# Newton's steps of the reciprocal square roots moved from VectorE to GpSimd, in a hybrid decoder layer

## The chip, the core and the metric

The kernel runs on one core of a Trainium2 chip. The time is device microseconds of one execution of the whole program, from a run on the chip; lower is better. The engines are named as in the profile: PE (TensorE matmuls), PEld (its weight loads), DVE (VectorE), ACT (ScalarE), POOL (GpSimd), SP (SyncE, which here issues DMAs). Each engine runs its own list of instructions in order, and engines wait for each other by semaphores.

## What is computed

One layer of a decoder trunk on 2048 tokens of width 1024, in float32. The input is normalised and multiplied by one wide weight matrix; the columns of the result feed five groups of four heads of 64; each group's output is gated, the five are joined (width 1280), multiplied by an output matrix and added to the input:

```
h = rms_norm(x, norm_g)
proj = h @ w_in
ya = spatial_gating(...)          # A: gMLP, with an rms_norm over each head of v
yb = forgetting_attention(...)    # B: softmax attention, rms_norm over each head of q and k
yc = mlstm(...)                   # C: chunked matrix memory, rms_norm over each head of its output
yd = rwkv7_time_mix(...)          # D: delta rule; a norm over each head of k, rms_norm of its output
ym = memory_attention(...)        # M: attention to 256 memory tokens, rms_norm of q and k
out = x + concat(y * silu(z)) @ w_out
```

Every one of these norms needs a reciprocal square root of a small statistic: `y * rsqrt(mean(y * y) + eps)`.

## The kernel before

Each float32 product is made of three passes of a split number (a rounded part and a rest), so the weights and the activations are first split by ACT (L222, L329: the rounded part) and DVE (L225, L330: the rest). The work comes in three stretches. From 0 to about 950 us PE runs the input projections (L267, L289, L315) in blocks of 512 tokens, with the recurrent groups C and D between them. From about 950 to 1430 us attention B and M runs beside the projections of group A and of M. From there to the end PE runs the output projection (L879).

The source is written as generators that are stepped between groups of matmuls, and a scheduler that works on the written program sets the final order of each engine's list. The order is fixed when the program is built; at run time each engine keeps to its list.

`rsqrt` (L148 to L156) turns a small tile `t` in place into its reciprocal root. Line 152 makes a first guess from the bits of `t`, and three rounds of Newton's method follow (L154, L155, L156), every step needing the one before. The tiles are 128x8 mostly, some 128x4, 128x2 or 64x16. All of it stands on DVE: ten instructions a call. The two helpers `rq` (the guess `y` and the scratch `u`) are single buffers that all calls share.

The calls, 62 in all:
- `rstd` (L369) and `first` (L502): the statistic `ss` of the layer's input and of the memory tokens; PE spreads it by L383, or ACT uses it (L749).
- `head_norm` (L403): the statistic `rs` of the heads of q and k (then L413 on DVE scales, and PE transposes in L418), of group C (then L1683 on DVE), and of group A (then L715 on DVE). L401 is the sum before it, on DVE, and L397 the square, on ACT.
- group D: `rn` in the front part (L1311; PE spreads it by L1322) and `sy` in the back part (L1497; L1510 on DVE scales).

POOL has little else. In the first stretch these are small copies (L632, L634, L1297, L1373) and two products in each of the eight front parts of group D (L1315, L1333). In attention it adds up the exponentials: ACT writes a tile `pe` (L1087), and POOL adds it to `es` (L1099 the first two, L1101 the others), one list of adds for every block of 512 queries.

Of the kernel before, what the change touches and what calls it, by code (L numbers as in the profile page):

```python
# [13 lines left out]
ALU = mybir.AluOpType  # L14
# [106 lines left out]
def body(ctx: ExitStack, tc, x, xT, mem, memT, wp, wkv, wout, pv, wa, sguT, sgub, out, dbg=None):  # L121
    nc = tc.nc
    V, A, G, T, SY = nc.vector, nc.scalar, nc.gpsimd, nc.tensor, nc.sync
# [24 lines left out]
    def rsqrt(t):  # L148

        n, b = t.shape[0], t.base_partition() if callable(t.base_partition) else t.base_partition  # L150
        y, u = (cp.tile([P, 16], F32, tag=f"rq{i}", bufs=1, name="rq")[b:b + n, :t.free_size()] for i in range(2))
        V.tensor_scalar(y.bitcast(I32), t.bitcast(I32), -0.5, 1597463007.0, op0=ALU.mult, op1=ALU.add)
        for o in (y, y, t):
            V.tensor_tensor(u, y, y, op=ALU.mult)  # L154
            V.scalar_tensor_tensor(u, u, -0.5, t, op0=ALU.mult, op1=ALU.mult)  # L155
            V.scalar_tensor_tensor(o, u, 1.5, y, op0=ALU.add, op1=ALU.mult)  # L156


    hp2 = cp.tile([P, 16], F32, name="hp2")
# [22 lines left out]
    rctx = ExitStack()  # L182
    rp = rctx.enter_context(tc.tile_pool(name="rp", bufs=1, side="right"))
    rwkv = Rwkv(nc, rp, dr, lambda: bank("rw"), bank, ident, par, hp2, rsqrt, wa, dd, smd, mixd[3])

    cw = ctx.enter_context(ExitStack())
# [164 lines left out]
    def rstd(pool, tags, src, ntile):  # L351

        ss = mp.tile([P, 2, 4], F32, tag="ss", bufs=2, name="ss")
        xts = deque()
        lag = len(tags)
        for i in range(2 * ntile + lag):
            if i >= lag:
                j, xt = i - lag, xts.popleft()
                A.activation(xt, xt, AF.Square, accum_out=ss[:, j % 2, j // 2:j // 2 + 1])
            if i < 2 * ntile:  # L360
                tag, bufs = tags[i % lag]
                xts.append(pool.tile([P, Q], F32, tag=tag, bufs=bufs, name="xt"))
                SY.dma_start(xts[-1], src(i // 2, slice(i % 2 * Q, (i % 2 + 1) * Q)))
            if i >= lag - 1:
                yield
        r = ss[:, 0, :ntile]
        V.tensor_tensor(r, r, ss[:, 1, :ntile], op=ALU.add)
        V.tensor_scalar(r, r, 1.0 / DM, EPS, op0=ALU.mult, op1=ALU.add)
        rsqrt(r)  # L369
        yield  # L370
        return ss[:, 0]
# [22 lines left out]
    def head_norm(pt, n, eps, pool=None):  # L394

        sq = pool.tile([P, 3 + Q], F32, tag="cext", bufs=2, name="sq") if pool else xp.tile([P, 512], F32, tag="sq", bufs=2, name="sq")
        A.activation(sq[:, :n], pt, AF.Square)  # L397
        yield
        m = n // HD
        r = xp.tile([P, 8], F32, tag="rs", bufs=4, name="rs")  # L400
        V.tensor_reduce(r[:, :m], sq[:, :n].rearrange("q (u x) -> q u x", x=HD), axis=AX.X, op=ALU.add)  # L401
        V.tensor_scalar(r[:, :m], r[:, :m], 1.0 / HD, eps, op0=ALU.mult, op1=ALU.add)
        rsqrt(r[:, :m])  # L403
        yield
        yield
        yield
        return r[:, :m].rearrange("q (u o) -> q u o", o=1).to_broadcast([P, m, HD])
# [434 lines left out]
    op = att.c4.enter_context(tc.tile_pool(name="op", bufs=2, side="right"))  # L842
# [912 lines left out]
```

## Time and profile before

| what | value |
|---|---|
| median of three runs | 1740.68 us (1735.09 to 2513.16) |
| the profiled execution's own time | 1736.49 us |
| its span, first to last instruction | 1734.8 us |
| granted TensorE clock, mean | 0.975 of full |
| PE / DVE / ACT / POOL busy | 95% / 69% / 51% / 17% of the span |
| instructions on DVE / POOL | 2990 / 356 |

Matmuls are pipelined and their ends are modelled, so a busy PE is not a PE at its peak. The profile's idle times name what ended them. Equal instructions can have quite different durations, and in a list that is kept in order an instruction that waits holds up all behind it.

### The profile page before, as it was taken

Reading aid. Unit: us, or ns where it says so; the run is one execution under the profiler, and the core shown is the slowest. Engines: PE = TensorE matmul, PEld = TensorE weight load, DVE = VectorE, ACT = ScalarE, POOL = GpSimd, SP = SyncE. Lnnn points to the kernel's source line nnn. Section 1 sums busy time; section 2 is a strip of 40 time slices with the busy share of each in tenths; the row PEclk is TensorE's granted clock in tenths of the full one; section 3 lists DMA queues with packets and bytes.
Section 4 is the critical chain, followed back from the end, with each engine's and each line's share of the span. In section 5 each row is a group of like instructions: output and inputs, shape, how many; then the busy total and the mean of one; then the engine's idle time right before and its main releaser. Section 6 shows DMA issues by size and latency. Waiting matters only on the chain.

```text
span 1734.8 us, 31669 instructions
## 1 busy us (share of the span) xinstructions
PE 1641.8 (95%) x11306; PEld 1282.2 (74%) x11306; DVE 1196.9 (69%) x2990; ACT 881.3 (51%) x1895; POOL 302.3 (17%) x356
## 2 busy tenths in 40 slices
PE   7898999799999999999999999999999988999999
PEld 5676778687978888798888766667656655677887
DVE  7678685685977679488676887788687786752220
ACT  5566554544555455555444756566465646631110
POOL 5010000010100101010000045344444242100000
PEclk9999999899999999999999989999999999999999
DMA  6878654542453443344334544334334425654441
GB/s 198 256 230 259 184 161 97 139 145 86 135 157 101 132 141 115 86 134 146 98 101 141 167 120 130 105 102 130 96 86 110 113 68 137 191 162 114 143 130 56
DMA packets 200151, 234.36 MB, mean 135 GB/s; under 512 B 75016, under 2 KB 107336, under 8 KB 199992
## 3 DMA queue, kind: packets, MB, share of 16 engines
q1 hardware_dynamic: 185144, 218.69, 43.7%
q10 hardware_dynamic: 14848, 13.64, 2.6%
q8 instruction: 89, 1.46, 0.4%
q14 instruction: 70, 0.57, 0.1%
HBM read 180.44 MB, written 51.81 MB: 134 GB/s over the span
## 4 chain that ended last, share of the span: by engine, by line
PE 64%; DVE 16%; DMA 11%; ACT 4%; issue 3%; POOL 1%; SPq 1%; ACTq 0%; DVEq 0%; POOLq 0%
PE pj L315 14%; PE pj L879 12%; PE pj L267 12%; PE acc L1108 4%; DMA wraw<-in_wp 4%; PE pj L289 4%; DVE wt L225 2%; PE wk L1026 2%; PE p L1082 2%; PE p L1085 2%; PE rw L1359 1%; PE rw L1482 1%; PE rw L1484 1%; DVE ht L330 1%; DVE mx L1040 1%
## 5 line engine op out<-in xcount | busy, mean ns | idle before, releaser
L267 PE MATMUL pj<-ht,wt 128*128 128x512 f32 x1632 | 422.6, 403 | 5.8 <-DVE ht L330 2.7
L267 PEld LDWEIGHTS pj<-ht,wt 128*128 128x128 f32 x1632 | 298.3, 190 | 84.5 <-issue 10.5
L315 PE MATMUL pj<-wt,ht 128*128 128x256 f32 x2400 | 332.7, 290 | 9.3 <-ACT wt L222 3.4
L315 PEld LDWEIGHTS pj<-wt,ht 128*128 128x128 f32 x2400 | 304.9, 193 | 27.5 <-issue 7.4
L225 DVE TENSOR_TENSOR wt<-wraw,wt 128x512 fp32r<-128x512 f32 (+1 forms) x312 | 217.6, 700 | 78.0 <-ACT wt L222 76.4
L222 ACT CAST wt<-wraw 128x512 fp32r<-128x512 f32 (+1 forms) x312 | 184.8, 601 | 140.2 <-DMA wraw<-in_wp 92.5
L879 PE MATMUL pj<-wo,mt 128*128 128x512 f32 x960 | 231.3, 398 | 1.8 <-ACT wo L830 1.8
L879 PEld LDWEIGHTS pj<-wo,mt 128*128 128x128 f32 x960 | 180.2, 189 | 47.2 <-issue 2.4
L1101 POOL TENSOR_TENSOR es<-es,pe 128x512 f32<-128x512 f32 (+3 forms) x128 | 153.7, 1201 | 103.9 <-ACT pe L1087 98.9
L289 PE MATMUL pj<-ht,wt 128*128 128x512 f32 x480 | 138.9, 426 | 13.3 <-ACT wt L222 11.7
L1087 ACT ACTIVATE pe<-p 128x512 f32<-128x512 f32 x192 | 100.3, 541 | 50.3 <-PE p L1085 43.9
L1040 DVE TENSOR_REDUCE mx<-wk 128x1 f32<-128x512 f32 (+3 forms) x192 | 111.8, 614 | 18.2 <-PE wk L1026 14.3
L289 PEld LDWEIGHTS pj<-ht,wt 128*128 128x128 f32 x480 | 91.8, 200 | 39.1 <-ACT wt L222 12.1
L1108 PE MATMUL acc<-pe,v 128*64 128x512 f32 (+3 forms) x384 | 104.0, 594 | 6.3 <-DVE at L1141 6.3
L329 ACT ACTIVATE ht<-xr,pvt 128x512 fp32r<-128x512 f32 (+1 forms) x88 | 61.4, 703 | 61.9 <-DMA xr<-hbd 29.2
L1099 POOL TENSOR_TENSOR es<-pe 128x512 f32<-128x512 f32 (+1 forms) x32 | 43.2, 1351 | 246.3 <-ACT pe L1087 200.3
L1026 PE MATMUL wk<-ka,qb 66*128 66x512 f32 (+3 forms) x224 | 73.2, 383 | 10.2 <-DVE mx L1040 9.7
L1082 PE MATMUL p<-qa,kb 128*128 128x512 f32 x192 | 75.8, 396 | 5.8 <-ACT pe L1087 5.8
L330 DVE SCALAR_TENSOR_TENSOR ht<-xr,pvt,ht 128x512 fp32r<-128x512 f32 (+1 forms) x88 | 68.4, 784 | 16.8 <-ACT ht L329 16.1
L859 ACT CAST mt<-mr 128x256 fp32r<-128x256 f32 x80 | 31.6, 406 | 94.1 <-DMA mr<-mix 50.3
L1026 PEld LDWEIGHTS wk<-ka,qb 66*128 66x128 f32 x224 | 41.0, 196 | 49.3 <-DVE mx L1040 19.5
L1085 PE MATMUL p<-qb,ka 68*128 68x512 f32 x192 | 75.4, 395 | 0.0
(332 smaller groups left out, 2423.1 us busy)
## 6 DMA issues: line engine op xcount, KB each, us to landing
wraw<-in_wp SPq DMA_DIRECT2D x288, 256.0 KB
xr<-hbd SPq DMA_DIRECT2D x56, 256.0 KB
mr<-mix SPq DMA_DIRECT2D x80, 128.0 KB
xr<-in_x SPq DMA_DIRECT2D x32, 256.0 KB
out<-xr ACTq DMA_DIRECT2D x32, 256.0 KB
xt<-in_x SPq DMA_DIRECT2D x24, 256.0 KB
xr<-in_xT SPq DMA_DIRECT2D x24, 256.0 KB
hbd<-xr SPq DMA_DIRECT2D x24, 256.0 KB
```

The lines of the kernel that those rows point to most:

```text
L222: A.copy(wt[:, :, 0, :ncol], raw[:, :, :ncol])
L225: V.tensor_tensor(lo, raw[:, :, :ncol], wt[:, :, 0, :ncol].bitcast(F32), op=ALU.subtract)
L267: T.matmul(pt, wt[k // 2][:, k % 2, a, m * P:(m + 1) * P], hts[k][:, b, :], start=n == 0, stop=n == 3 * KT - 1)
L289: T.matmul(pts[m], wt[k // 2][:, k % 2, a, m * P:(m + 1) * P], hts[k][:, b, :], start=k + n == 0, stop=k == KT - 1 and n == 2)
L315: T.matmul(pt[:, ii * 256:ii * 256 + 256], hts[k][:, a, (i + ii) * P:(i + ii + 1) * P], wt[k // 2][:, k % 2, b, :], start=n == 0, stop=n = ...
L879: T.matmul(po, mts[i // 2, k][:, a, i % 2 * P:(i % 2 + 1) * P], wo[e * NK + k][:, b], start=n == 0, stop=n == 3 * NK - 1)
L1026: T.matmul(p1, self.qb[0:66, i * P:(i + 1) * P], self.k[kk][0][0:66, :w], start=True, stop=True, skip_group_check=diag)
L1040: V.tensor_reduce(*late.pop(), axis=AX.X, op=ALU.max)
L1082: T.matmul(p2[:, f:], kb[:, ks], self.qa[:, f:], start=True, stop=False)
L1085: T.matmul(p2[:, f:], ka[:, ks], self.qb[:, f:], start=False, stop=True)
L1101: G.tensor_tensor(self.sum[:, f:], self.sum[:, f:], e[:, f:], op=ALU.add)
L1108: self.att.nc.tensor.matmul(self.acc[64 * i:64 * i + 64, f:], self.v[:, kt], e[:, f:], start=kt < 2, stop=True, skip_group_check=True)
```

## The change

In `rsqrt` the first guess stays on DVE. The three rounds go to POOL, and since a round is written there as products and one multiply-add with two constants, it has four instructions instead of three: the square of the guess, its product with `t`, times -0.5 plus 1.5, and the product with the guess. A call is then one instruction on DVE and twelve on POOL.

```diff
         V.tensor_scalar(y.bitcast(I32), t.bitcast(I32), -0.5, 1597463007.0, op0=ALU.mult, op1=ALU.add)
         for o in (y, y, t):
-            V.tensor_tensor(u, y, y, op=ALU.mult)
-            V.scalar_tensor_tensor(u, u, -0.5, t, op0=ALU.mult, op1=ALU.mult)
-            V.scalar_tensor_tensor(o, u, 1.5, y, op0=ALU.add, op1=ALU.mult)
+            G.tensor_tensor(u, y, y, op=ALU.mult)
+            G.tensor_tensor(u, u, t, op=ALU.mult)
+            G.tensor_scalar(u, u, -0.5, 1.5, op0=ALU.mult, op1=ALU.add)
+            G.tensor_tensor(o, u, y, op=ALU.mult)
```

Lines below this place have a number that is higher by one in the changed kernel (L413 becomes L414). The scheduler makes a new order of the whole program. Three places of it follow.

DVE, at two calls of `head_norm` for q and k (tiles `rs` and `yn`) in the last block of the projections. Before:

```order
L152 TENSOR_SCALAR rq<-rs 128x8
L638 SCALAR_TENSOR_TENSOR qk<-cext,pvt,qk 128x512
L154 TENSOR_TENSOR rq<-rq 128x8
L1402 COPY xs<-x_125 128x256
L155 SCALAR_TENSOR_TENSOR rq<-rq,rs 128x8
L638 SCALAR_TENSOR_TENSOR qk<-cext,pvt,qk 128x512
L156 SCALAR_TENSOR_TENSOR rq<-rq 128x8
L154 TENSOR_TENSOR rq<-rq 128x8
L155 SCALAR_TENSOR_TENSOR rq<-rq,rs 128x8
L156 SCALAR_TENSOR_TENSOR rq<-rq 128x8
L154 TENSOR_TENSOR rq<-rq 128x8
L642 SCALAR_TENSOR_TENSOR qk<-cext,qk 128x512
```

And now:

```order
L402 TENSOR_REDUCE rs<-sq 128x8
L403 TENSOR_SCALAR rs<-rs 128x8
L152 TENSOR_SCALAR rq<-rs 128x8
L402 TENSOR_REDUCE rs<-sq 128x8
L403 TENSOR_SCALAR rs<-rs 128x8
L152 TENSOR_SCALAR rq<-rs 128x8
L414 TENSOR_TENSOR yn<-yn,rs 128x512 x2
L331 SCALAR_TENSOR_TENSOR ht<-xr,pvt,ht 128x512
L226 TENSOR_TENSOR wt<-wraw,wt 128x2x256 x2
```

The nine steps that lay among other work are gone from DVE. The scaling of `yn`, which needs their result, stands right behind the first guess of a second call, and that one needs the shared `rq` back from the first call.

POOL, near the end of attention, where it adds exponentials. Before:

```order
L1099 TENSOR_TENSOR es<-pe 128x512 x5
L1101 TENSOR_TENSOR es<-es,pe 128x512 x11
L1101 TENSOR_TENSOR es<-es,pe 128x384
L1101 TENSOR_TENSOR es<-es,pe 128x256
L1101 TENSOR_TENSOR es<-es,pe 128x128
L1099 TENSOR_TENSOR es<-pe 128x512 x3
```

And now:

```order
L154 TENSOR_TENSOR rq<-rq 128x8
L1102 TENSOR_TENSOR es<-es,pe 128x512
L155 TENSOR_TENSOR rq<-rq,rs 128x8
L1102 TENSOR_TENSOR es<-es,pe 128x512
L156 TENSOR_SCALAR rq<-rq 128x8
L157 TENSOR_TENSOR rq<-rq 128x8
L154 TENSOR_TENSOR rq<-rq 128x8
L155 TENSOR_TENSOR rq<-rq,rs 128x8
L156 TENSOR_SCALAR rq<-rq 128x8
L157 TENSOR_TENSOR rq<-rq 128x8
L1102 TENSOR_TENSOR es<-es,pe 128x512
L154 TENSOR_TENSOR rq<-rq 128x8
```

The steps of one call now stand in one list with the adds, and some adds stand between them.

PE, at the first front part of group D, where the statistic `rn` is spread over partitions. Before:

```order
L1300 MATMUL wk<-smp,w2r 128x256 x2
L1308 MATMUL wk<-bones,ag 128x2 x4
L278 MATMUL pj<-ht,wt 128x512
L267 MATMUL pj<-ht,wt 128x512 x30
L1322 MATMUL wk<-ident,rn 64x128 x8
L267 MATMUL pj<-ht,wt 128x512 x18
```

And now:

```order
L1309 MATMUL wk<-bones,ag 128x2 x4
L279 MATMUL pj<-ht,wt 128x512 x2
L268 MATMUL pj<-ht,wt 128x512 x11
L1323 MATMUL wk<-ident,rn 64x128
L268 MATMUL pj<-ht,wt 128x512 x4
L1323 MATMUL wk<-ident,rn 64x128 x4
L268 MATMUL pj<-ht,wt 128x512 x2
L1323 MATMUL wk<-ident,rn 64x128 x3
```

Between the sums that `rn` is made of and its first use 31 projection matmuls stood, and now 13 do.

## Rows read from the trace of the kernel before

**Rows 1.** The page, busy time of each engine, share of the span, instructions.

```profile
PE 1641.8 (95%) x11306; PEld 1282.2 (74%) x11306; DVE 1196.9 (69%) x2990; ACT 881.3 (51%) x1895; POOL 302.3 (17%) x356
```

**Rows 2.** The page, the chain that ended last, by engine.

```profile
PE 64%; DVE 16%; DMA 11%; ACT 4%; issue 3%; POOL 1%; SPq 1%; ACTq 0%; DVEq 0%; POOLq 0%
```

**Rows 3.** Stretches: busy us and instructions by engine, clock, DMA.

```profile
0.00:950.00 950.00, 897.72 (x7404) 745.41 (x7405) 696.16 (x2035) 501.88 (x1132) 93.04 (x184) 0.98 0.50 147
950.00:1430.00 480.00, 453.25 (x2543) 318.79 (x2543) 375.84 (x712) 284.59 (x557) 187.54 (x156) 0.96 0.41 113
```

**Rows 4.** Stretches, DVE busy with tile rq: all ten steps of the calls.

```profile
0.00:950.00 950.00, 82.98 (x460) 0.98 0.50 147
950.00:1430.00 480.00, 61.82 (x160) 0.96 0.41 113
```

**Rows 5.** Stretches, DVE busy with line L152 alone.

```profile
0.00:950.00 950.00, 7.57 (x46) 0.98 0.50 147
950.00:1430.00 480.00, 3.83 (x16) 0.96 0.41 113
```

**Rows 6.** Timeline of DVE, an undisturbed call: start, us, instruction.

```profile
281.16 0.17 DVE L152 TENSOR_SCALAR rq<-rs 128x8 int32<-128x8 int32 x1
281.37 0.17 DVE L154 TENSOR_TENSOR rq<-rq 128x8 f32<-128x8 f32 x1
...
283.17 0.69 DVE L413 TENSOR_TENSOR yn<-yn,rs 128x512 f32<-128x512 f32 x1
```

**Rows 7.** Timeline of DVE and POOL, a call in attention.

```profile
1419.63 1.12 DVE L154 TENSOR_TENSOR rq<-rq 128x8 f32<-128x8 f32 x1
1420.79 0.17 DVE L155 SCALAR_TENSOR_TENSOR rq<-rq,rs 128x8 f32<-128x8 f32 x1
...
1417.14 4.98 POOL L1101 TENSOR_TENSOR es<-es,pe 128x512 f32<-128x512 f32 x3 [6.61 <-ACT pe L1087]
```

**Rows 8.** Timeline of POOL: small and large, alone and dependent.

```profile
459.91 0.19 POOL L632 COPY cext<-ccy 128x3 f32<-128x3 f32 x1 [2.54 <-DVE rs L401]
1084.21 1.29 POOL L1101 TENSOR_TENSOR es<-es,pe 128x512 f32<-128x512 f32 x1 [0.51 <-ACT pe L1087]
1090.37 0.45 POOL L1101 TENSOR_TENSOR es<-es,pe 128x128 f32<-128x128 f32 x1 [2.11 <-ACT pe L1087]
1098.70 1.10 POOL L1099 TENSOR_TENSOR es<-pe 128x384 f32<-128x384 f32 x1 [1.49 <-ACT pe L1087]
1099.88 0.74 POOL L1101 TENSOR_TENSOR es<-es,pe 128x256 f32<-128x256 f32 x1
```

**Rows 9.** Groups by line and form: count, busy us, mean ns, idle before.

```profile
L632 POOL COPY cext<-ccy 128x3 f32<-128x3 f32 x16 | 7.5, 474 | 45.0 <-DVE qk L642 39.8 <-DVE rs L401 5.2
L225 DVE TENSOR_TENSOR wt<-wraw,wt 128x512 fp32r<-128x512 f32 x296 | 213.2, 723 | 78.0 <-ACT wt L222 76.4
L426 ACT COPY yn<-pj 128x512 f32<-128x512 f32 x24 | 14.0, 582 | 15.9 <-PE pj L315 11.7 <-DMA qk_Bk<-yn 4.1
L397 ACT ACTIVATE sq<-yn 128x512 f32<-128x512 f32 x25 | 15.8, 630 | 0.4
L401 DVE TENSOR_REDUCE rs<-sq 128x8 f32<-128x512 f32 x41 | 27.7, 680 | 17.1 <-ACT sq L397 16.9
L402 DVE TENSOR_SCALAR rs<-rs 128x8 f32<-128x8 f32 x41 | 12.1, 294 | 0.5
L413 DVE TENSOR_TENSOR yn<-yn,rs 128x512 f32<-128x512 f32 x25 | 18.0, 718 | 0.5
```

**Rows 10.** The chain that ended last: start, us, what.

```profile
861.51 11.10 PE pj L267 x48
```

**Rows 11.** Waits from 950 to 1430 us: total, times, longest.

```profile
POOL es L1099 <- ACT pe L1087: 98.4, 13, 10.6
POOL es L1101 <- ACT pe L1087: 97.0, 67, 6.6
```

**Rows 12.** Waits of PE: total us, times, longest.

```profile
PE wk L1322 <- DVE rn L156: 5.1, 5, 1.5
PE wk L418 <- DVE yn L413: 3.7, 4, 1.4
```

## The prediction

> **What bounds the kernel now.** I began with the page. PE is busy for 95% of the span and DVE for 69%, while POOL is busy for 17% [rows 1]. The reader should see an engine that is nearly full, a second one with a third of its time free, and a third one that is mostly empty. The chain of work that ended last is PE for 64% and DVE for 16% of the span; POOL has 1% [rows 2]. So time that is taken from DVE shows at the end only in part, and I use that 16% as its price below. The stretches show where there is room: PE has 52 us without work among the first 950 us and 27 us in attention, and POOL's 188 us in attention are 39% of that stretch, where the new work meets the most of its old work [rows 3].
>
> **What leaves DVE.** Nine of the ten steps of 62 calls. All ten steps take 83.0 us before 950 us and 61.8 us in attention [rows 4]; the first guesses, which stay, are 7.6 and 3.8 of that [rows 5]. So 75.4 and 58.0 us go, 133.4 us together. That is 0.16 us a step (75.4 over 9 x 46) in the first stretch, and 0.40 us (58.0 over 9 x 16) in attention. The reason is in two timelines. An undisturbed call runs at one step in 0.2 us, so nine steps last 1.8 us [rows 6]. In attention a step of the same size took 1.12 us while POOL was adding exponentials, and the next, 0.17 us [rows 7].
>
> **What POOL pays for a step.** POOL has no row of a product of 128x8, so I bound it. From below: a copy of three columns took 0.19 us, and the adds of 128 and of 512 columns, 0.45 and 1.29 us, lie on a line of 2.2 ns a column that begins at 0.17 and gives 0.19 us for 8 columns. A dependent add began 0.08 us after the end of the one before (1098.70 plus 1.10 is 1099.80, and the next starts at 1099.88) [rows 8]. That makes 0.27 us a step, 3.2 us for twelve, and 3.4 with a handover of 0.1 us on either side. No row has a multiply-add on POOL; I give it the price of the others. From above: the 16 copies of three columns took 0.47 us in the mean, beside a DVE that works on products of 0.72 us [rows 9]. That makes 0.55 us a step and 6.8 us a call. I take 4.5 us, near the low end: 3.4 plus three waits of half a product of DVE, 0.36 us each. The low end is nearer because DVE itself comes to a stop at the result, and from then on POOL works undisturbed.
>
> The Trainium skill, GPSIMD Engine Reference, section Engine selection, says that elementwise work belongs on VectorE, GPSIMD being about twice as slow with two inputs. Twice the 0.17 us of a DVE step would give a call of 6.3 us as an estimate, and by what follows an end near 1765 us. The trace bears the factor out for long operands (1.29 against 0.72 us for 512 columns) and not for the short copy (0.19 us), so I keep 4.5.
>
> **What DVE pays instead.** It now waits for POOL, in its own list. I went through the 62 calls in the new order and added up, by the mean durations of the trace, what DVE has to do between a first guess and whatever needs POOL next: the result, or the single shared `rq` for the next call's guess. Such a second guess comes after less than 4 us of other work in 13 calls (6 before); the DVE excerpt above has one. With a call of 4.5 us DVE arrives early in 32 of the 46 calls of the first stretch, by 93 us together, and in 14 of 16 in attention, by 48 us. Twelve adds of L1101 and two of L1099 stand between steps of these sixteen calls, for 14 x 1.37 = 19 us more (1.29 plus 0.08 [rows 8]). So DVE waits 93 + 48 + 19 = 160 us in place of 133 us of work: 27 us more, of which 16% is 4 us at the end. With 3.4 us a call the waits are 58 + 33 + 19 = 110 us, 23 us less than the work, which is 4 us off the end. With 6.8 us they are 169 + 82 + 19 = 270 us, 137 us more, or 22 us at the end. Behind a waiting DVE stand the splitting of weights (L225), that of activations (L330) and, in attention, the maxima; PE waits for all of these.
>
> **What PE pays.** In attention its order is the same. In the projections it comes to some users of the result earlier. At the first front part of group D 13 matmuls of 0.231 us [rows 10] are left, 3.0 us, to cover two small DVE steps, the call and a handover, some 5.0 us: PE waits 2 us. The other seven fronts keep at least 6.5 us of cover. For q and k the way from the projection's end is a copy, a square, a sum, its scaling, a guess, the call and the product: 0.58 + 0.63 + 0.68 + 0.29 + 0.17 + 4.5 + 0.72 = 7.6 us [rows 6, 9], and the shortest cover left is 8.3 us. That does, except where two calls stand close: at the place shown the second one starts 3.6 us late, so PE waits 3 us. The waits of before at these users, 5.1 and 3.7 us [rows 12], stay as they are. POOL itself gains 62 x 3.2 = 200 us of work, to about 29% of the span; its adds have 195 us of waiting for exponentials in attention to hide 16 calls in [rows 11].
>
> **The sum.** 1736.5 us, the profiled execution's own time, plus 4 for DVE, 2 and 3 for PE: 1746 us. It is 0.3% over the median of the runs, 1740.7, which the profiled execution lies 0.2% under. A measurement of this kernel can tell about 2%, so the bounds are 1706 and 1775 us.
>
> **Rivals.**
>
> *Slower by adds that wait.* POOL keeps its order, so a step of the call behind an add waits for that add's exponential, and ACT gets it from PE, and PE may stand still for the maxima or weights that DVE holds back while it waits for POOL. This is the circle that wasn't there before. An add of L1101 waited 97.0/67 = 1.4 us, one of L1099 98.4/13 = 7.6 us [rows 11]. Twelve and two of them inside calls, and one ahead of each of 16 calls, make 17 + 15 + 23 = 55 us. If all of it reaches the end, that is 1801 us; it is slower by 2% from 30 us on, if more than half gets through. For it speaks that 14 of 16 calls leave DVE nothing to do; against it, that POOL's waits are for work of engines that mostly do not wait for DVE just then. Chance 0.14.
>
> *Slower by the port.* Steps of two inputs on DVE and POOL hold each other up [rows 7]; if it happens at every step, a call is 6.8 us. Then DVE gives 22 us, the first front 4, and q and k about 10, since 9.9 us of way meet 8.3 to 10 us of cover: 1773 us. The Trainium skill, SBUF — State Buffer, section SBUF: two separate sides, says that the port pair that GPSIMD shares with VectorE is locked for a whole instruction against a VectorE one with two SBUF inputs, and the second to come waits; the 1.12 us step beside an add agrees with it. Against this case speaks that DVE runs out of products soon. Chance 0.17.
>
> *Faster.* DVE has 538 us without work, and if its new waits fall into time that it would have idled anyway, the relief counts alone: 16% of 133 us is 21 us, so 1715 us; with half of PE's 27 us in attention too, 1702. For it speaks that the relief is densest there (0.40 us a step); against it, that the excerpts show the waits right ahead of work that PE needs. Chance 0.15.
>
> *The forecast*, one late engine in place of another, from about 1728 to 1762 us, has 0.54. That the steps remain on DVE can be excluded: the order shows them on POOL.
>
> **The numbers.** The range takes in the low and the high call (1735 and 1773 with the PE terms), most of the faster rival and the lower half of the first: 1716 to 1778 us. Over 1775 lie 0.11 of the first rival, 0.07 of the second and 0.01 of the forecast: 0.19. Under 1706 lie 0.08 of the third and 0.01: 0.09. The rest is 0.72.
>
> **What would show it.** DVE busy falls by 100 to 135 us, and a new wait of DVE for POOL's `rs`, `sy` and `rq` of 110 to 270 us appears. POOL shows 744 steps, of 0.19 to 0.47 us in the mean. PE waits for `rn` at the first L1323. Small DVE steps over 1 us in attention are gone, but for L402. The prediction is wrong if a step on POOL costs over 0.55 us with its gap, or if DVE's waits sum to much over 270 us (the first rival), or if PE's idle time in attention falls by over 10 us (the third).

## The result, and the profile after

The changed kernel takes 1853.99 us (median of 4 runs, 1846.94 to 1857.88) beside 1739.89 us before: a ratio of 1.0649, interval 1.0612 to 1.0686. That is 114 us slower; the forecast of 1746 was 6 us. The profiled execution took 1854.53 us, its span is 1852.8. Ratios, here and below, are formed from the fast runs alone (one execution of the kernel before took 2513 us), so they can differ a little from the quotient of two medians.

The page, busy time by engine, answers to [rows 1]:

```profile
PE 1691.8 (91%) x11306; PEld 1316.8 (71%) x11306; DVE 1116.3 (60%) x2432; ACT 880.8 (48%) x1895; POOL 493.6 (27%) x1100
```

DVE has 80.6 us less to do, POOL 191.3 us more. PE runs the same 11306 matmuls, is busy 50.0 us longer and stands idle 161.0 us in place of 93.0. These two make the 118 us by which the span grew. The mean granted clock fell from 0.975 to 0.946 of the upper level, 2.4 GHz, or 3%, and the mean of the largest group of matmuls (L267, now L268) rose from 403 to 415 ns, also 3%. In this run PE stands idle longer, is granted less clock, and pays a second time; the wait at 846 us below shows one such fall of the clock.

The chain that ended last, by engine, answers to [rows 2]:

```profile
PE 50%; DVE 14%; DMA 12%; POOL 10%; issue 7%; ACT 5%; SPq 1%; ACTq 0%; POOLq 0%; DVEq 0%
```

PE held 64% of the chain, and now 50%. POOL went from 1% to 10%. Its steps are part of what sets the end.

The stretches of [rows 3], after the change (columns as there; the same times, but less of the program is done in them):

```profile
0.00:950.00 950.00, 855.46 (x6566) 702.54 (x6567) 604.77 (x1499) 461.29 (x1035) 217.37 (x640) 0.94 0.47 138
950.00:1430.00 480.00, 441.83 (x2803) 324.92 (x2801) 314.39 (x569) 265.33 (x537) 202.34 (x364) 0.95 0.39 110
```

In the first 950 us PE ends 6566 matmuls in place of 7404. The first attention score (L1082, now L1083) starts at 1073 us in place of 977, 96 us late; the output projection (L879, now L880) starts at 1590 in place of 1477, 113 us late. So most of the loss arises before attention.

Tile `rq` after the change: the steps on POOL (durations in ns: least, median, most), and who waited for a result of a call. It answers to [rows 4, 6, 7, 8]:

```profile
L154 POOL TENSOR_TENSOR rq<-rq x186: 188/199/1824, 21.3 to 1539.2; 128x8 f32<-128x8 f32 x147, 64x16 f32<-64x16 f32 x24, 128x4 f32<-128x4 f32 x12, 128x2 f32<-128x2 f32 x3
L156 POOL TENSOR_SCALAR rq<-rq x186: 189/197/827, 21.9 to 1539.7; 128x8 f32<-128x8 f32 x147, 64x16 f32<-64x16 f32 x24, 128x4 f32<-128x4 f32 x12, 128x2 f32<-128x2 f32 x3
...
L155 POOL TENSOR_TENSOR rq<-rq,rs x123: 199/202/1856, 296.6 to 1539.5; 128x8 f32<-128x8 f32 x123
...
  DVE yn L414: 48.1, 16
  DVE gv L716: 32.9, 8
  DVE rq L152: 22.0, 11
  DVE to L1684: 14.4, 6
...
  PE wk L384: 12.3, 3
...
  DVE x L1511: 10.4, 4
...
  PE wk L1323: 7.2, 2
```

A step is 0.20 us, products and multiply-adds alike. DVE waited 127.8 us for roots or for the shared `rq` (48.1 + 32.9 + 22.0 + 14.4 + 10.4), and PE 19.5 us for roots that it reads itself. I call the sum, 147.3 us, the **root waits**. In the kernel before DVE made the roots in its own list, and PE waited 5.1 us for those that it reads itself, at L1322 [rows 12].

PE's waits that grew most (total us, times, longest; they answer to [rows 12]):

```profile
PE wk L419 <- DVE yn L414: 20.5, 8, 6.5
PE wk L1027 <- DVE mx L1041: 19.7, 16, 3.5
PE wk L384 <- POOL ss L157: 12.3, 3, 7.2
...
PE wk L1323 <- POOL rn L157: 7.2, 2, 4.7
```

L419 waited 3.7 us before. The longest of these waits shows how a late root reaches PE. Timeline of the changed kernel (start, us, instruction, idle before it and what ended it):

```profile
837.86 0.20 POOL L157 TENSOR_TENSOR rn<-rq 128x8 f32<-128x8 f32 x1
838.01 0.50 POOL L1298 COPY gc<-L 64x8 f32<-64x8 f32 x2
838.10 0.17 DVE L152 TENSOR_SCALAR rq<-rs 128x8 int32<-128x8 int32 x1 [1.50 <-POOL rn L157]
...
838.57 0.53 POOL L633 COPY cext<-ccy 128x3 f32<-128x3 f32 x1
...
839.06 1.28 POOL L1316 TENSOR_TENSOR th<-th,kl 128x512 f32<-128x512 f32 x1
...
840.31 0.64 POOL L154 TENSOR_TENSOR rq<-rq 128x8 f32<-128x8 f32 x1
...
844.28 0.20 POOL L157 TENSOR_TENSOR rs<-rq 128x8 f32<-128x8 f32 x1
...
844.51 1.21 DVE L152 TENSOR_SCALAR rq<-rs 128x8 int32<-128x8 int32 x1 [2.91 <-POOL rs L157]
...
845.75 0.68 DVE L414 TENSOR_TENSOR yn<-yn,rs 128x512 f32<-128x512 f32 x1
...
846.57 1.08 PE L419 MATMUL wk<-ident,yn 128*128 128x128 f32 x4 [6.54 <-DVE yn L414]
```

Three calls stand close together. The guess of the second waits for `rq`; its steps then wait on POOL for 2.2 us of older work (L1298, L633, L1316); the guess of the third, two places ahead of `yn` in DVE's list, waits for the second; and PE stands still for 6.54 us. The stretch right behind this pause (columns as in [rows 3]) shows PE at work without a break and at half the clock:

```profile
846.60:850.00 3.40, 3.40 (x22) 2.74 (x23) 1.19 (x4) 1.71 (x3) 2.54 (x11) 0.50 0.45 133
```

In the 3.1 us before the pause the granted clock was 1.00, 2.4 GHz; here it is 0.50, 1.2 GHz; and from 851.3 to 855 us it is 1.00 again. In the kernel before, the steps at this place lay among other work of DVE. Its timeline:

```profile
786.00 0.68 DVE L413 TENSOR_TENSOR yn<-yn,rs 128x512 f32<-128x512 f32 x1
786.60 0.15 DVE L154 TENSOR_TENSOR rq<-rq 128x8 f32<-128x8 f32 x1
786.68 0.17 DVE L1406 TENSOR_TENSOR xtmp<-xs,at 128x24 f32<-128x24 f32 x1
786.77 0.74 DVE L330 SCALAR_TENSOR_TENSOR ht<-xr,pvt,ht 128x512 fp32r<-128x512 f32 x1
787.44 0.15 DVE L155 SCALAR_TENSOR_TENSOR rq<-rq,rs 128x8 f32<-128x8 f32 x1
```

A step lasts 0.15 us, but the next, independent instruction starts 0.08 us after it. So the recorded durations overlap, and here a step between other work costs DVE half of its duration.

### The profile page after: what moved, and what is told of

It reads as the page before. It is cut to its first block, busy times and chain, and to the rows that moved or that the text cites. A ratio compares the mean times of both kernels' runs of the same rounds, so it can differ in the third digit from the quotient of the medians.

```text
span 1852.8 us, 31868 instructions
## 1 busy us (share of the span) xinstructions
PE 1691.8 (91%) x11306; PEld 1316.8 (71%) x11306; DVE 1116.3 (60%) x2432; ACT 880.8 (48%) x1895; POOL 493.6 (27%) x1100
## 4 chain that ended last, share of the span: by engine, by line
PE 50%; DVE 14%; DMA 12%; POOL 10%; issue 7%; ACT 5%; SPq 1%; ACTq 0%; POOLq 0%; DVEq 0%
PE pj L880 12%; PE pj L268 10%; PE pj L316 8%; PE acc L1109 4%; DMA wraw<-in_wp 3%; PE pj L290 3%; DVE wt L226 2%; POOL rq L154 2%; POOL rq L156 2%; POOL rq L155 2%; PE wk L1027 2%; PE p L1083 1%; POOL rq L157 1%; DMA ao<-dn 1%; PE p L1086 1%
## 5 line engine op out<-in xcount | busy, mean ns | idle before, releaser
L268 PE MATMUL pj<-ht,wt 128*128 128x512 f32 x1632 | 441.4, 415 | 8.8 <-ACT ht L330 5.0
L268 PEld LDWEIGHTS pj<-ht,wt 128*128 128x128 f32 x1632 | 308.5, 197 | 92.7 <-issue 12.1
L316 PE MATMUL pj<-wt,ht 128*128 128x256 f32 x2400 | 338.7, 294 | 12.2 <-DVE wt L226 4.2
L316 PEld LDWEIGHTS pj<-wt,ht 128*128 128x128 f32 x2400 | 310.9, 197 | 30.6 <-issue 7.4
L226 DVE TENSOR_TENSOR wt<-wraw,wt 128x512 fp32r<-128x512 f32 (+1 forms) x312 | 227.2, 733 | 99.6 <-ACT wt L223 98.5
L880 PE MATMUL pj<-wo,mt 128*128 128x512 f32 x960 | 234.3, 401 | 1.6 <-ACT wo L831 1.6
L880 PEld LDWEIGHTS pj<-wo,mt 128*128 128x128 f32 x960 | 182.3, 192 | 47.7 <-issue 3.1
L290 PE MATMUL pj<-ht,wt 128*128 128x512 f32 x480 | 139.0, 427 | 9.2 <-ACT wt L223 7.4
L154 POOL TENSOR_TENSOR rq<-rq 128x8 f32<-128x8 f32 (+3 forms) x186 | 55.0, 296 | 306.7 <-DVE rq L152 291.1
L290 PEld LDWEIGHTS pj<-ht,wt 128*128 128x128 f32 x480 | 92.4, 201 | 34.0 <-ACT wt L223 7.4
L1083 PE MATMUL p<-qa,kb 128*128 128x512 f32 x192 | 77.1, 402 | 9.6 <-ACT pe L1088 9.6
```

The source lines that it names most:

```text
L226: V.tensor_tensor(lo, raw[:, :, :ncol], wt[:, :, 0, :ncol].bitcast(F32), op=ALU.subtract)
L268: T.matmul(pt, wt[k // 2][:, k % 2, a, m * P:(m + 1) * P], hts[k][:, b, :], start=n == 0, stop=n == 3 * KT - 1)
L290: T.matmul(pts[m], wt[k // 2][:, k % 2, a, m * P:(m + 1) * P], hts[k][:, b, :], start=k + n == 0, stop=k == KT - 1 and n == 2)
L316: T.matmul(pt[:, ii * 256:ii * 256 + 256], hts[k][:, a, (i + ii) * P:(i + ii + 1) * P], wt[k // 2][:, k % 2, b, :], start=n == 0, stop=n = ...
L880: T.matmul(po, mts[i // 2, k][:, a, i % 2 * P:(i % 2 + 1) * P], wo[e * NK + k][:, b], start=n == 0, stop=n == 3 * NK - 1)
L1083: T.matmul(p2[:, f:], kb[:, ks], self.qa[:, f:], start=True, stop=False)
```

## The experiments

Three theories. **A**: the waits for the roots cost the time. **B**: POOL's steps and DVE's products hold each other up. **C**: the new order of the lists costs it, whatever the engine of the steps. Ratios are to runs of the kernel before on the same chip; microseconds made from them use 1742 us. Differences under 2% stand on the intervals alone, which are given behind each ratio.

**Half of the calls.** Calls before attention, or those in it, stay on DVE:

```
E = G if late[0] == 1 else V        # att_pool; == 0 in proj_pool
# late[0] becomes 1 where attention opens
```

> The sixteen calls of the attention stretch on POOL, the 46 earlier ones on DVE with three instructions a round as before. Theory A (the result comes late, and what DVE loses while it waits goes on to PE almost in full): the two traces put 28 us of the 118 into attention, so 1740 + 28 = 1768 us, with DVE stalled for about 55 us there. Theory B (the port: POOL's steps lengthen DVE's and the reverse): POOL is busiest in attention, so most of the loss would be here, 1800 us or more. Theory C (the loss comes from another order of the work, whatever the engine of the calls): the earlier stretch would keep part of its loss, since the lists are built in one piece: over 1790 us.

> The 46 calls before attention on POOL, the sixteen of attention on DVE as before. Theory A: 1740 + 90 = 1830 us, with about 94 us of stalls of DVE and PE idle about 50 us more than before. Theory B: the smaller part of the loss, under 1800 us. If the two halves do not add up to 118 us within 15, the stretches are not independent, which speaks for theory C.

att_pool: 1756.37 us, ratio 1.009 (1.0058 to 1.0122). proj_pool: 1826.87 us, 1.0492 (1.0452 to 1.0531). The loss lies in the projections, where POOL had little other work (93 of 950 us), which speaks against B as I had put it. att_pool lost 16 us of the 28 that I expected by A; proj_pool came as expected (1830). The halves make 5.8% of the 6.5%, 12 us short of the whole and inside the 15 us beyond which I would have taken it as a sign of C.

**What DVE work is worth.** Five rounds on DVE, two rounds on DVE, and no round at all:

```
for o in (y, y, y, y, t):           # dve5, rounds of three steps on V
for o in (y, t):                    # two_rounds_dve
V.tensor_scalar(t.bitcast(I32), ...)  # no_newton: the guess goes straight into t
```

> All on DVE, five rounds in place of three, so 6 x 62 = 372 DVE steps more and no POOL step: some 50 us of DVE work in the first stretch (46 x 6 x 0.18) and 40 in attention. It prices DVE time without any wait for POOL. By the 16% of the prediction: 1740 + 0.16 x 90 = 1754 us. By theory A in its strict form (a us of DVE ahead of work that PE needs is a us at the end): 1800 us or more. If it comes under 1760 us, a us of DVE work is cheap, and what is dear is a wait at these places alone.

> All three rounds are left out: a call is the first guess alone, on DVE (the roots are then good to a few per cent). It shows what the relief of DVE is worth when no wait is put in its place: 133 us of DVE work less than before. By the 16% of the prediction: 1740 - 21 = 1719 us. If the relief is worth nothing, because PE is the bound in those places: 1735 to 1740 us. If a us of DVE is worth a us: under 1650 us, PE's idle 93 us being the most that can go, so about 1650 us.

> The kernel before with two rounds on DVE in place of three (the last round is left out): a third of the relief of the run without any rounds (18 us for nine steps), so 1742 - 6 = 1736 us. It is the way to relieve DVE of Newton's steps without any wait, and by theory A it should beat both kernels; if the relief came only from the whole call going, 1740 us.

no_newton: 1724.74 us, 0.990 (0.9874 to 0.9926); two rounds: 1750.41 beside 1749.64 us, 1.0007 (0.9989 to 1.0025); five rounds: 1774.78 us, 1.0189 (1.0159 to 1.0219). The busy line of no_newton:

```profile
PE 1639.7 (95%) x11306; PEld 1286.7 (75%) x11306; DVE 1116.7 (65%) x2432; ACT 880.9 (51%) x1895; POOL 304.2 (18%) x356
```

All of the relief is worth 17 us, 13% of the 133 us of step durations. So the prediction's price of 16% was near for the whole relief. A third of it is worth nothing that could be measured: my guess of 6 us was a miss. Work that is added costs more than work that is taken away gives: five rounds cost 33 us (I had expected 14 by the 16%) for the 54.8 us by which they raised DVE's busy time, 1251.7 in place of 1196.9. That is 60%, without any wait for POOL. In no_newton DVE has the same 2432 instructions as in the changed kernel, and is as busy to 0.4 us; the two runs are 129 us apart.

No_newton also bears on B. DVE's larger groups by form, in the changed kernel (count, busy us, mean ns, idle before):

```profile
L226 DVE TENSOR_TENSOR wt<-wraw,wt 128x512 fp32r<-128x512 f32 x296 | 222.3, 756 | 99.5 <-ACT wt L223 98.5
...
L414 DVE TENSOR_TENSOR yn<-yn,rs 128x512 f32<-128x512 f32 x25 | 21.5, 859 | 48.1 <-POOL rs L157 48.1
...
L716 DVE TENSOR_TENSOR gv<-gv,rs 128x512 f32<-128x512 f32 x8 | 10.0, 1254 | 32.9 <-POOL rs L157 32.9
```

And in no_newton, with no step on POOL:

```profile
L226 DVE TENSOR_TENSOR wt<-wraw,wt 128x512 fp32r<-128x512 f32 x296 | 221.1, 751 | 105.8 <-ACT wt L223 104.3
...
L414 DVE TENSOR_TENSOR yn<-yn,rs 128x512 f32<-128x512 f32 x25 | 19.1, 763 | 0.3
...
L716 DVE TENSOR_TENSOR gv<-gv,rs 128x512 f32<-128x512 f32 x8 | 9.4, 1174 | 0.2
```

The weight split lasted 723 ns before [rows 9], 756 in the changed kernel, and 751 with POOL out of it. So the longer products came with the steps leaving DVE, not with their arrival on POOL, and the half of B in which POOL holds up DVE falls as a cause of the 114 us.

The other half is there. POOL's steps in the changed kernel, the most frequent form of each line:

```profile
L154 POOL TENSOR_TENSOR rq<-rq 128x8 f32<-128x8 f32 x147 | 44.5, 302 | 237.2 <-DVE rq L152 224.1 <-DVE rs L403 5.1
L156 POOL TENSOR_SCALAR rq<-rq 128x8 f32<-128x8 f32 x147 | 35.7, 243 | 12.3
```

Their means are 302 and 243 ns, their medians 0.20 us. Of all 744 steps the trace has 100 of over 0.3 us, every one beside an instruction of DVE, while the 485 that ran beside none took 0.20 us in the mean. The 744 took 194.6 us, 45 us more than at 0.20 us each: 0.7 us a call. By the price of a round, below, that may be 20 to 35 us of the 114 (an estimate; no run has calls that DVE leaves alone). It reaches the end through the length of the call, so it is a part of A's waits and not beside them.

**The length of a call.** Two rounds and four on POOL:

```
for o in (y, t):                    # pool2
for o in (y, y, y, t):              # pool4
```

> The changed kernel with two rounds on POOL in place of three (the last round is left out): four steps of 0.28 us less in each call, 1.1 to 1.3 us, DVE's list unchanged in length. Theory A (a us of waiting of DVE is 0.8 to 0.9 us at the end; the two runs with the same DVE work, 1853.99 with 150 us of waits and 1724.74 without, give 129 of 150): about 45 calls wait, so 50 to 60 us of waits go and the time is about 1805 us. Theory C (the order of the lists costs the time, not the waits): 1840 to 1855 us. By the 16% of the prediction: 1845 us.

> The changed kernel with four rounds on POOL: 1.1 to 1.3 us more a call. Theory A: nearly all of the 62 calls wait now, so 65 to 75 us more of waits, and 1854 + 60 = 1914 us. Theory C: 1854 us within 15. By the 16%: 1865 us. Together with two and three rounds it gives the slope of the time in the length of a call.

pool2: 1787.72 us, 1.029 (1.0242 to 1.0338); pool4: 1893.01 us, 1.0904 (1.0845 to 1.0962). Against the three rounds' 1.0649 a round is worth 63 us and 44 us. DVE's two largest root waits with two rounds:

```profile
DVE yn L414 <- POOL rs L157: 31.1, 17, 3.4
...
DVE gv L716 <- POOL rs L157: 17.9, 7, 4.2
```

With four:

```profile
DVE yn L414 <- POOL rs L157: 66.4, 20, 6.8
...
DVE gv L716 <- POOL rs L157: 36.6, 7, 7.8
```

From the end of the guess to the end of the last step a call takes 3.2, 4.6 and 6.1 us with two, three and four rounds. The time follows the length of the call, as A has it; by the 16% a round would have been 11 us at most (62 calls of 4 x 0.28 us).

**Where the users stand.** The four products that use a root, put behind all DVE work written before them, in the changed kernel and, as its control, in the kernel before:

```
pin = tc.keep_in_program_order
pin(V.tensor_tensor(y3, y3, r, op=ALU.mult))   # and v3, yv, h3
```

> The changed kernel with one difference in the order alone: the four products that use a result are placed on DVE behind all DVE work that is written before them in the program, so more work stands between a guess and its user. By my sum over the order, DVE has some 60 to 70 us of waits less than the changed kernel. Theory A: 1854 - 0.85 x 65 = about 1800 us, if PE does not wait for the later yn instead. Theory that PE needs the result itself (a late yn, gv) and not what DVE holds back: no gain, 1850 to 1900 us.

> The control for the run with later users: the same four products placed behind the DVE work written before them, with the calls on DVE as before the change. Theory A: nothing waits for POOL here, so the placement has nothing to cover: 1740 us within 10. If it is faster by 20 us or more, that much of the 73 us which the placement took off the changed kernel has nothing to do with POOL.

users_later: 1781.12 us, 1.0233 (1.018 to 1.0287). The control: 1763.41 beside 1749.64 us, 1.009 (1.0058 to 1.0122), slower than the kernel before by itself, which I had not expected. In this order the move to POOL costs 1.4% in place of 6.5%. The root waits of DVE that are left:

```profile
DVE rq L153 <- POOL rs L158: 15.1, 8, 3.2
...
DVE yn L415 <- POOL rs L158: 12.8, 6, 2.9
...
DVE to L1685 <- POOL rs L158: 5.2, 2, 3.2
...
DVE rq L153 <- POOL sy L158: 3.8, 2, 2.5
...
DVE gv L717 <- POOL rs L158: 2.6, 1, 2.6
```

With 1.0 us for `rn` they make 40.5 us in place of 127.8. The same calls, as long as before (5.1 us in the mean), cost a fifth when other work stands between guess and user.

**The products on POOL.** Nobody on DVE waits for `rs` any more, but the product itself comes later:

```
G.tensor_tensor(y3, y3, r, op=ALU.mult)        # and v3, h3
```

> The changed kernel with the products that use the result (yn and gv of the fronts, the division's product of group D) on POOL too, so that DVE does not wait for the result there: the waits of 48, 33 and 14 us are gone, those for the shared scratch (22) and for the combined output (10) stay. Theory A with DVE as the one that suffers: 1740 + 45 = 1785 us. If PE suffers because the result itself is late (yn goes straight to PE's transposes), the time stays at 1840 us or rises, as a POOL product of 512 columns takes about 1.3 us or more in place of 0.72. Theory B (port): more two-input work on POOL, slower than 1854 us.

1821.74 us, 1.0464 (1.0423 to 1.0505): under half of the 69 us that I gave it at best. PE took the wait over:

```profile
PE wk L419 <- POOL yn L414: 30.3, 9, 5.5
...
PE wk L1323 <- POOL rn L157: 14.8, 3, 10.1
```

DVE's root waits are 35.9 us, PE's 55.8 (with `yn`, which POOL now makes). A late result costs by either way.

**The shared scratch**, a second pair that every other call of up to eight columns uses:

```
alt[0] ^= 1
w, k = (8, "rp") if alt[0] and t.free_size() <= 8 else (16, "rq")
```

> The changed kernel with a second pair of scratch columns that every other call of up to eight columns uses, so that the next guess need not wait for the last call on POOL. In the changed kernel DVE waited 22 us in 11 guesses for the shared pair. Theory A: about half of that goes (two calls in line on POOL still follow each other, and the next product waits instead): 1854 - 10 = 1844 us; if the shared pair held back more than the waits show, 1830 us or less.

1847.66 us, 1.0558 (1.053 to 1.0586), where the changed kernel had 1.0649. DVE's waits at the guess fell from 22.0 to 6.2 us, those at `yn` rose from 48.1 to 54.1. The scratch is a small part.

**All that shortens the waits together**, with two rounds on POOL:

> All that shortens the waits together, with the steps still on POOL: later users, a second scratch pair, two rounds in place of three (the last round is left out). Theory A: the waits of 108 us with later users become about 45, and at 0.5 to 0.85 us for each the time is 1781 - 35 to 1781 - 55, about 1730 to 1745 us: level with the kernel before. If it stays over 1760 us, something other than the waits is left.

1761.56 beside 1749.64 us, 1.006 (1.0038 to 1.0082), with 26.9 us of root waits (12.5 of DVE, 14.4 of PE). On the scale of 1742 us that is 1752, and I had expected 1730 to 1745, level with the kernel before: something besides these waits is left, and the placement costs 0.9% by itself (the control). Beside that control, which has three rounds on DVE, the move with two rounds costs nothing that could be measured: it is not bad in itself.

**The same order without the waits.** In the runs so far the scheduler made another order, slightly or widely. This one nearly keeps the changed kernel's (in the traces 2197 of DVE's 2432 instructions and 11038 of PE's 11306 stand at the same place) and takes the waits alone away:

```
V.tensor_scalar(t.bitcast(I32), t.bitcast(I32), -0.5, ...)  # users read the guess
... # POOL's twelve steps work from t on columns that nobody reads
tc.add_manual_dep(user.ins, last.ins.name, NoSync)  # place in the list, no wait
```

> The changed kernel's order, with every POOL step in its place, but nobody waits for them: the first guess goes straight to the users, and POOL's twelve steps a call work from it on columns that nobody reads (the roots are then good to a few per cent, and one factor of the steps is 1). The users keep their places behind the steps in the order alone. 9023 of PE's 9228 and 2201 of DVE's 2435 instructions stand at the very position that they have in the changed kernel. Theory A (the waits cost the time): 1725 to 1735 us, as without any rounds. Theory C (the new order costs it): 1820 to 1855 us. Theory B (POOL's steps disturb DVE's): in between, and DVE's other lines longer than in the run without rounds, by as much as in the changed kernel or more.

1762.1 beside 1746.59 us, 1.0093 (1.006 to 1.0125): between the theories, and much nearer to A. Its busy line:

```profile
PE 1657.4 (94%) x11306; PEld 1296.0 (74%) x11306; DVE 1109.4 (63%) x2432; ACT 881.4 (50%) x1895; POOL 538.2 (31%) x1100
```

POOL is busier than in the changed kernel, DVE and PE's lists are nearly the same, and 97 us of the 114 are gone. The weight split is no longer than in no_newton, with all 744 steps on POOL:

```profile
L238 DVE TENSOR_TENSOR wt<-wraw,wt 128x512 fp32r<-128x512 f32 x296 | 220.2, 749 | 112.6 <-ACT wt L235 111.8
```

It stays 1.9% or 34 us above no_newton. What differs is the order, and older work of POOL that now stands behind the steps:

```profile
DVE bk L1347 <- POOL th L1331: 21.7, 6, 6.4
```

This wait was not among those of the kernel before; in the changed kernel it was 11.8 us. How the 34 us are shared between order and POOL's queue was not separated.

The root waits, by DVE plus PE, and the ratios, in order:

| run | root waits, us | ratio |
|---|---|---|
| no_newton | 0 | 0.990 |
| steps_unwaited | 0 | 1.0093 |
| later_2nd_2rounds | 12.5 + 14.4 | 1.006 |
| users_later | 40.5 + 21.5 | 1.0233 |
| pool2 | 79.3 + 11.2 | 1.029 |
| user_on_pool | 35.9 + 55.8 | 1.0464 |
| second_scratch | 114.6 + 18.6 | 1.0558 |
| the change | 127.8 + 19.5 | 1.0649 |
| pool4 | 163.2 + 38.7 | 1.0904 |

The ratios rise with the root waits but for small steps; steps_unwaited, with none, lies above the line, as order and queue would have it. No version that keeps at least two rounds is faster than the kernel before by a margin that can be measured.

## Why the prediction was wrong

**The failed step is the price.** The prediction set waits against work, "160 us in place of 133 us of work: 27 us more, of which 16% is 4 us at the end". The two have different prices. The work that left was worth 17 us (no_newton), 13%, near the share of the chain. The waits cost 97 us (the change less steps_unwaited, 1.0649 - 1.0093), two thirds of the 147.3 us of root waits, where the prediction's 16% of 160 us is 26. What steps_unwaited has over no_newton, 34 us, goes with the new order and POOL's queue, for which the sum had no term. The three make -17 + 34 + 97 = 114 us, as they must, being the steps from one ratio to the next.

Why the share of the chain came near for the work and not for the waits is argued, not shown: it is a mean over DVE's work, and in the kernel before the steps were spread between other work (the timeline at 786 us), while a wait stands in one place, directly ahead of the user of the root, and what PE needs next stands behind it. Nor is it the waiting as such that is dear. Steps added on DVE, with no wait for POOL, cost 60% of DVE's new busy time (dve5), close to the waits' two thirds. What the share of the chain priced was time taken from DVE; time added in a call was dearer in both forms.

**What was right.** The steps: predicted 0.27 us with the gap at the low end, measured 0.20 and 0.08 where nothing disturbs them. The call: 4.5 us predicted, 4.67 in the mean over 46 calls before 1040 us and 4.97 over 16 in attention, from the start of the guess to the end of the last step. The waits of DVE in its list, 93 us before attention and 67 in it: 76.0 and 51.8 measured (before and after 1040 us), 127.8 in place of 160. The places, too: `yn`, `gv`, the next guess. The mechanism was the forecast's own, a late engine in place of a busy one; its size was taken from the wrong row.

**What was mis-sized besides.** The relief: 133 us of durations were only 80 us of busy time, since a step between independent work overlaps with its neighbours. PE's waits: 2 us for L1322 and 3 us for q and k. At L1322 the sum came out by luck: 5.1 us became 7.2, but the wait at the first front alone is 4.7 us, in place of 0.7, and three of the five waits of before are gone. L418 alone rose by 16.8 us, and the 12.3 us at L384, a root that PE reads directly, were in no term at all. I had looked at the fronts' covers and at those of q and k, and not at the four statistics `ss`. Nor did the sum have the second payment: 50 us of the 118 are matmuls that ran slower at the lower clock. With two levels, 1.00 and 0.50, a mean of 0.946 is an estimated 200 us at the lower one, where 0.975 was 87; half of the difference, 57 us, is near those 50. One reading of the rows is wrong besides: 75.4 us over 9 x 46 steps is 0.18 us a step, not 0.16; no term of the sum used it.

**The rivals.** *Adds that wait* asked for the loss in attention; it was 16 us of 114 there (att_pool). *The port* asked for calls of 6.8 us; they are 4.7 to 5.0. Single steps do show it: at 840.31 in the timeline a product of POOL took 0.64 us in place of 0.20. The Trainium skill, SBUF — State Buffer, section SBUF: two separate sides, tells of the lock between the two engines; these single steps agree with it. Over the run it does not lengthen DVE's products (no_newton), but the 45 us by which POOL's steps are longer are in the calls' 4.7 to 5.0 us. *Faster* gave the relief alone, 1715 us; no_newton is that kernel, and took 1724.74.

The Trainium skill, GPSIMD Engine Reference, section Engine selection, would not have moved this work, because GPSIMD is about twice as slow with two inputs. The outcome agrees, the reason in part: a step of 0.20 us is close to DVE's 0.17, but twelve steps with their gaps take 3.4 us where DVE's nine took 1.8 [rows 6], and a longer call costs time (pool2, pool4). Most of the loss came from who has to wait for it.

## What to carry to other kernels

Price what a change takes from an engine and what it adds there apart. For work that goes, the engine's share of the chain was near the mark here, and for a third of that work it was too much. For a wait, or for work added in the same places, look at what stands behind it in the list and who needs that, and count up to the full length of it. A result that is moved to another engine needs other work between its start and its first user; here where that work was placed was worth more (6.5% became 1.4% over its control) than a round less in the call (2.9%). And add what PE's clock costs when a change makes PE pause.

## What the runs showed of the hardware

On POOL, products and multiply-adds of 128 by 2 to 8 columns and 64 by 16 take 0.19 to 0.22 us when undisturbed, with 0.08 us between dependent ones. Beside an instruction of DVE 100 of the 744 took over 0.3 us, up to 1.86. DVE starts the next, independent instruction 0.07 to 0.08 us before the end of a step, so busy time falls by less than the durations that go (80 of 133 us). Over whole runs PE's busy time for the same 11306 matmuls went with the mean granted clock, with some scatter: 1639.7 us at 0.976 (no_newton), 1664.8 at 0.962 (pool2), 1691.8 at 0.946 (the change) but 1683.8 at the same 0.946 (user_on_pool), 1695.5 at 0.938 (pool4). Behind a pause of PE of 6.54 us the granted clock was 0.50, where it had been 1.00 ahead of it.
